# Attention stage of a two-layer hybrid block: a third score buffer, and two PSUM banks for everything else

## The chip, the core and the metric

The kernel runs on one core of a Trainium2 chip. The core has TensorE (PE in the profile; PEld is its weight load), VectorE (DVE), ScalarE (ACT), GpSimd (POOL) and SyncE (SP, which issues the loads and stores here). They run side by side, each through its own queue in order, and wait for each other by semaphores. PE writes its results into PSUM, eight banks of 512 fp32 columns by 128 partitions; DVE and ACT read them from there. The metric is the device time of one execution in microseconds (us), lower is better.

## What is computed

Two layers over 512 latent and 256 context tokens of width 1024. The part that matters here is the attention of head group B (four heads, two softmax maps each) and the output projection behind it, which also takes the results of groups A and C:

```
def diff_attn(q, k, v, lam):
    s = jnp.einsum("bqhmd,bkhmd->bhmqk", q.astype(F32), k.astype(F32)) * (B_QK_DIM ** -0.5)
    p = jax.nn.softmax(s, axis=-1)
    a = p[:, :, 0] - lam * p[:, :, 1]
    return jnp.einsum("bhqk,bkhd->bqhd", a, v.astype(F32))
...
def mixer_merge(pa, o, pc, P, lam_init):
    ya = chunk_gmlp(pa, P)
    yb = (rms_norm(o, P["subln_g"]) * (1.0 - lam_init)).astype(pa.dtype).reshape(b, n, B_WIDTH)
    yc = conformer_conv(pc, P)
    return jnp.concatenate([ya, yb, yc], axis=-1) @ P["w_out"]
...
    x_lat = x_lat + g1 * mixer_merge(pa, o, pc, P, lam_init)
```

Latent queries see 768 keys (latent and context); context queries, in layer 0 only, see the 256 context keys.

## The kernel before

Each layer goes through four stages: input projections with groups A and C; attention with the first part of the output projection; the rest of the output projection with the second norm; the gated feed-forward network. The change is in the attention stage (lines 766 to 922).

**Units and pairs.** A pair is one head with 256 queries, a unit one half of it (128 queries). Layer 0 has four small pairs on the context (256 keys) and eight large ones (768 keys), layer 1 the eight large ones. `q_prep` turns the queries of a pair on PE (tile `pq`) and splits them into a high part `qh` (ACT and POOL) and a remainder `ql` (DVE; the tile is called `qlz`). `scores` makes two score tiles per unit, one for each softmax map: four matmuls into `pss` (two banks, 1024 columns), then the row maximum on DVE (L825) and the exponential with its sum on ACT (L97, tile `e`). `combine` joins the two maps on DVE (L841). `transp` turns the result in blocks of 128 on PE into `pat` (a tile of four blocks and one of two), which ACT (L858) and DVE (L860) copy to `ath`. `attn_v` multiplies with the values into `po` (L870), and `subln` makes the norm's sum on PE (`pr`, L882), two small ACT steps and the scaled result `yB`, again as a high part and a remainder. Units are staggered: the transposes come two units behind the scores, `po` three, `pr` five.

**Fills.** The output projection sums over the results of A and C (`yAC`) and of B (`yB`). The share of `yAC` is known before the attention. So for `NFILL` = 2 (layer 0) and 3 (layer 1) blocks of 256 output columns, `wout` with parts (0,) computes it inside the attention stage: groups of twelve matmuls (four blocks of the sum, three products of high and low parts each, lines 275 to 277) into a bank `wo`, then one DVE update of the residual `xT` (L758). The segments are the 256 context tokens (layer 0 only) and the 512 latent ones, so a matmul of a fill has 256 or 512 columns. They come last in the program's text, so a scheduler that goes by priority puts them where PE would otherwise have nothing ready. The first group of layer 0 is written ahead of the attention. Their weights are loaded by SP and split into a high part `whi` (ACT) and a remainder `wlo` (POOL or DVE) in two buffers each; the first two blocks of layer 1 may come split already from DRAM (`wh`, `wl`).

**PSUM.** Eight banks: two score buffers of two banks (tag "s"), three banks for `pq`, `pat`, `po` and `pr` (tag "w", `WB`), one for the fills (tag "f", `FB`). A tile waits until the last reader of its bank's previous tile is done.

The order of each engine's instructions is set before the run by the scheduler, from priorities and free buffers; on the chip each engine goes through it strictly.

Of the kernel before, what the change touches and what calls it, by code (L numbers as in the profile page):

```python
# [9 lines left out]
F32 = mybir.dt.float32  # L10
# [6 lines left out]
P = 128  # L17
# [27 lines left out]

FB, WB, EB, QB = 1, 3, 5, 3
MRB, MRW, RAWB, NSQ, NTB, KXB, FTB = 4, 2, 3, 2, 3, 3, 2

HP, SCP, RSP = 1000, 2, 60
# [25 lines left out]
def tile_backbone(  # L77
# [18 lines left out]
    def act(out, in_, func, **kw):  # L96
        r = S.activation(out, in_, func, **kw)  # L97
        tab["since"].append(r.ins)
        tc.add_manual_dep(r.ins, tab["load"].name, NOSYNC, reason="activation table order")
        return r  # L100
# [13 lines left out]
    def psum_pool(stack, name):  # L114
        return stack.enter_context(tc.tile_pool(name=name, bufs=1, space=PSUM, reuse_waits="tile"))
# [99 lines left out]
    def wsplit(src, shape, eng="mix", raw=None, p=None, tags=("hi", "lo"), bufs=2):  # L215
        raw = raw or wload(src, shape)
        hi, lo = [(p or wp).tile([P] + shape, F32R, tag=t, name="w" + t, bufs=bufs) for t in tags]
        lo_n[0] += 1
        with tc.high_priority(offset=400):
            S.copy(hi, raw)  # L220
            e = V if eng == "dve" else G if eng == "pool" or lo_n[0] % 2 else V
            sub_lo(lo, raw, hi, e)
        return hi, lo
# [39 lines left out]
    def wsplit_of(key, src, shape, eng, tags=("hi", "lo"), p=None, **kw):  # L263
        if key not in split:
            return wsplit(src, shape, eng, p=p, **kw)
        r = []
        for x, t in enumerate(tags):
            w = (p or wp).tile([P] + shape, F32R, tag=t, name="w" + "hl"[x], bufs=RAWB if t == "raw" else 2)
            flat = w.rearrange("p a n -> p a n") if len(shape) == 2 else w.rearrange("p a k m -> p a (k m)")
            nc.sync.dma_start(out=flat.bitcast(F32), in_=split[key][:, x])  # L270
            r.append(w)
        return r

    def mm3(o, lhi, llo, rhi, rlo, start, stop):
        T.matmul(o, lhi, rhi, start=start, stop=False)  # L275
        T.matmul(o, lhi, rlo, start=False, stop=False)  # L276
        T.matmul(o, llo, rhi, start=False, stop=stop)  # L277
# [54 lines left out]
    for l in range(DEPTH):  # L332
# [5 lines left out]
        whole = [GL] if last else [GC_, GL]  # L338
# [20 lines left out]
        with ExitStack() as ph:  # L359
            sac = ExitStack()  # L360
            sp = pool(sac, f"s1_{l}", side)
            ps = psum_pool(ph, f"ps1_{l}")
# [380 lines left out]
        def wout_w(mp2, parts, eng, **kw):  # L743
            return [(wsplit_of(("out", q, mp2), w_out[l, q, mp2], [2, 4, P], eng, **kw), (yACh, yACl) if q == 0 else (yBh, yBl))
                    for q in parts]

        def wout(mp2, parts, w, segs, psf, tag, bufs, only=(0, 1)):

            for g in segs:
                a, b, s = g  # L750
                for i in only:
                    m = 2 * mp2 + i
                    o = psf.tile([P, 512], F32, tag=tag, name="wo", bufs=bufs)
                    for n, ((wh, wl), (yh, yl)) in enumerate(w):
                        for k in range(4):
                            mm3(o[:, :b - a], wh[:, i, k], wl[:, i, k], yh[:, k, a:b], yl[:, k, a:b],
                                n == 0 and k == 0, n == len(w) - 1 and k == 3)
                    V.scalar_tensor_tensor(  # L758
                        out=xT[:, m, a:b], in0=o[:, :b - a], scalar=modv[:, l, s, 2, m:m + 1],
                        in1=xT[:, m, a:b], op0=ALU.mult, op1=ALU.add)  # L760
                    if 1 in parts:
                        for h in ngs:
                            if h[0] >= a and h[1] <= b:
                                norm.add(m, h)

        with ExitStack() as ph:
            sp = pool(ph, f"s2_{l}", side)
            ps = psum_pool(ph, f"ps2_{l}")
# [16 lines left out]
            def q_prep(n):  # L785
                h, p = pairs[n]
                qh = sp.tile([P, 2, 256], F32R, tag="qh", name="qh", bufs=QB)
                ql = qlz[n % 2]
                pq = ps.tile([P, 256], F32, tag="w", name="pq", bufs=WB)
                for i in range(2):  # L790
                    T.transpose(pq[:, i * P:(i + 1) * P], qt[2 * p + i][:, h * P:(h + 1) * P], ident)
                if n == 0:
                    for m in range(2):
                        for a in range(2):
                            S.copy(qh[a * QKD:(a + 1) * QKD, m], pq[m * QKD:(m + 1) * QKD])
                    for m in range(2):
                        ms = slice(m * QKD, (m + 1) * QKD)
                        sub_lo(ql[ms, m], pq[ms], qh[ms, m])
                else:
                    qn = sp.tile([P, 256], F32R, tag="qn", name="qn", bufs=2)  # L800
                    S.copy(qn, pq)
                    for m in range(2):
                        src = qn[m * QKD:(m + 1) * QKD]
                        for a in range(2):
                            (G.tensor_copy if a else S.copy)(qh[a * QKD:(a + 1) * QKD, m], src)
                    for m in range(2):
                        ms = slice(m * QKD, (m + 1) * QKD)
                        sub_lo(ql[ms, m], pq[ms], qn[ms])
                st["q", n] = (qh, ql)

            def scores(n, i):
                h, p = pairs[n]
                k0, nk = (0, 6) if p < 2 else (LAT, 2)
                qh, ql = st["q", n]
                e = []
                sm = sp.tile([P, 2], F32, tag="sm", name="sm", bufs=4)
                for m in range(2):
                    pss = ps.tile([P, 1024], F32, tag="s", name="pss", bufs=2)
                    for (a, b) in ([(0, 512), (512, 768)] if p < 2 else [(0, 256)]):
                        ksl = slice(k0 + a, k0 + b)  # L820
                        qs = slice(i * P, (i + 1) * P)
                        T.matmul(pss[:, a:b], qh[:, m, qs], kk[:, 2 * h + m, ksl], start=True, stop=False)
                        T.matmul(pss[:, a:b], ql[:, m, qs], kk[:, 2 * h + m, ksl], start=False, stop=True)  # L823
                    mx = sp.tile([P, 1], F32, tag="mx", name="mx", bufs=4)
                    V.tensor_reduce(out=mx, in_=pss[:, :nk * P], op=ALU.max, axis=AX.X, negate=True)  # L825
                    em = sp.tile([P, TOK], F32, tag="e", name="e", bufs=EB)
                    act(em[:, :nk * P], pss[:, :nk * P], AF.Exp, bias=mx, accum_out=sm[:, m:m + 1])
                    e.append(em)
                st[n, i] = (e, sm)
# [61 lines left out]
            if l == 0:  # L891
                w0 = wout_w(0, (0,), "pool")
                g, i = first.pop(0)
                wout(0, (0,), w0, [g], ps, "f", FB, (i,))
            q_prep(0)
            nu = len(units)
            for u in range(nu + 8):
                if u < nu:
                    n, i = units[u]
                    if i == 0 and n + 1 < len(pairs):  # L900
                        with tc.high_priority(offset=SCP):
                            q_prep(n + 1)
                    with tc.high_priority(offset=SCP):
                        scores(n, i)
                    combine(n, i)
                v = u - LAG[0]
                if 0 <= v < nu:
                    transp(*units[v])
                v = u - LAG[1]
                if 0 <= v < nu and units[v][1] == 1:  # L910
                    attn_v(units[v][0])
                v = u - LAG[2]
                if 0 <= v < nu and units[v][1] == 1:
                    subln(units[v][0])

            for mp2 in range(NFILL[l]):
                if mp2 == 0 and l == 0:
                    for g, i in first:
                        wout(0, (0,), w0, [g], ps, "f", FB, (i,))
                else:  # L920
                    wout(mp2, (0,), wout_w(mp2, (0,), "pool"), whole, ps, "f", FB)
        kvs.close()


# [9 lines left out]
        with ExitStack() as ph:  # L934
            pss_ = ctx.enter_context(ExitStack())
            ps = psum_pool(pss_, f"ps3_{l}")
# [18 lines left out]
            for x in range(len(todo) + 1):  # L955
# [3 lines left out]
                if x < len(todo):  # L959
                    mp2, w, i = todo[x]  # L960
# [8 lines left out]
        with ExitStack() as ph:  # L969
# [22 lines left out]
            for half in range(2):  # L992
                gh = hp.tile([P, HJ, toks], F32R, tag="gh", name="gh", bufs=1)
                gl = hp.tile([P, HJ, toks], F32R, tag="gl", name="gl", bufs=1)
                for jj in range(HJ):
# [3 lines left out]
                    w = [wsplit(w_gv[l, j, g], [KD, P], "dve") for g in range(2)]  # L999
# [43 lines left out]
                for mp2 in range(KD // 2):  # L1043
                    tail = half == 1 and mp2 == KD // 2 - 1
                    ws = {}
                    for gi, gs in enumerate([[g] for g in ngs] if tail else [whole]):
                        pd = {g: [ps.tile([P, 512], F32, tag="acc", name="pd", bufs=8) for i in range(2)] for g in gs}
                        cs_ = chunks[::-1] if gi else chunks
                        for ci, (j0, jn) in enumerate(cs_):
# [4 lines left out]
                            for jj in range(jn):  # L1054
# [3 lines left out]
                                for g in gs:  # L1058
                                    a, b, s = g
# [4 lines left out]
                        for g in gs:  # L1064
                            a, b, s = g
# [109 lines left out]
```

## Time and profile before

| | |
|---|---|
| median of 3 runs | 1602.82 us (1602.46 to 1603.99) |
| the profiled execution | 1602.73 us, of which its span 1600.4 |
| PE busy in the span | 1565.2 us (98%), 8186 matmuls |
| DVE busy | 1016.0 us (63%) |
| ACT busy | 643.3 us (40%) |
| POOL busy | 113.3 us (7%) |
| attention of layer 0, from the first pq to the last pr | 244.3 to 349.2 us |
| attention of layer 1 | 1108.8 to 1191.7 us |

The span runs from the first to the last instruction. A matmul's row shows its own duration, which overlaps the next one's; the step from one start to the next is what PE spends on it. DVE and ACT rows overlap a little in the same way. In a row of the timeline, brackets at the end name idle time just before it and what ended it.

### The profile page before, as it was taken

To read this page: it belongs to the slowest core of one execution; us is meant where nothing else is said; L and a number is where in the kernel's file an instruction comes from. 1 tells how busy PE (TensorE), PEld (TensorE's weight loads), DVE (VectorE), ACT (ScalarE), POOL (GpSimd) and SP (SyncE) were. 2 spreads that over 40 slices of the span, in tenths; PEclk is the share of its full clock that TensorE was granted. 3 is DMA by queue.
4 is the path that set the end of the run, shared out by engine and by line. 5 is a ranking of instruction groups with operands and counts; after the bars stand their busy time and mean duration, and the time that the engine had idled before them with its cause. 6 is when DMAs were issued, how large, how long until landed. Compare 5 with 4: busy or idle time off the path is not lost.

```text
span 1600.4 us, 21118 instructions
## 1 busy us (share of the span) xinstructions
PE 1565.2 (98%) x8186; PEld 1289.8 (81%) x8186; DVE 1016.0 (63%) x1713; ACT 643.3 (40%) x1115; POOL 113.3 (7%) x128
## 2 busy tenths in 40 slices
PE   6999998999999999999999999999999999999999
PEld 4875776778788888888888887887778888888888
DVE  4497968969999982145444354996977444334433
ACT  5431568762532221124333233255765333123321
POOL 1130124310000000000000000001320000000000
PEclk9999999999999999999999999999999999999999
DMA  7625210015265872116666476642011323332232
GB/s 282 216 68 183 62 54 27 14 40 198 68 196 185 284 257 74 63 66 198 209 192 207 152 272 221 202 157 93 14 42 54 103 95 96 89 103 92 92 108 90
DMA packets 76372, 208.77 MB, mean 130 GB/s; under 512 B 11504, under 2 KB 13808, under 8 KB 76144
## 3 DMA queue, kind: packets, MB, share of 16 engines
q1 hardware_dynamic: 76272, 207.43, 40.0%
q8 instruction: 64, 1.05, 0.3%
q14 instruction: 36, 0.29, 0.1%
HBM read 183.28 MB, written 24.12 MB: 130 GB/s over the span
## 4 chain that ended last, share of the span: by engine, by line
PE 91%; DVE 4%; ACT 4%; issue 1%; DMA 0%; POOL 0%; POOLq 0%; DVEq 0%; SPq 0%; ACTq 0%
PE pp L276 13%; PE pp L275 13%; PE pp L277 13%; PE pd L277 6%; PE pd L276 6%; PE pd L275 6%; PE acc L443 5%; PE acc L451 5%; PE acc L444 5%; PE po L870 3%; PE wo L275 2%; PE wo L276 2%; PE wo L277 2%; PE mr L156 2%; ACT e L97 1%; PE accC L496 1%
## 5 line engine op out<-in xcount | busy, mean ns | idle before, releaser
L220 ACT CAST whi<-raw 128x1024 fp32r<-128x1024 f32 (+1 forms) x174 | 178.4, 1027 | 510.3 <-PE pp L276 248.4
L276 PE MATMUL pp<-hlo,whi 128*128 128x512 f32 (+1 forms) x1072 | 380.6, 356 | 0.8 <-DVE hlo L316 0.8
L275 PE MATMUL pp<-hhi,whi 128*128 128x512 f32 (+1 forms) x1072 | 379.8, 356 | 1.5 <-ACT whi L220 1.3
L277 PE MATMUL pp<-hhi,wlo 128*128 128x512 f32 (+1 forms) x1072 | 379.0, 355 | 0.0
L106 DVE TENSOR_TENSOR wlo<-raw,whi 128x1024 fp32r<-128x1024 f32 (+2 forms) x159 | 191.4, 1206 | 287.9 <-ACT whi L220 280.3
L275 PEld LDWEIGHTS pp<-hhi,whi 128*128 128x128 f32 x1072 | 201.3, 188 | 35.2 <-ACT whi L220 2.7
L276 PEld LDWEIGHTS pp<-hlo,whi 128*128 128x128 f32 x1072 | 201.4, 188 | 32.8 <-DVE hlo L316 1.5
L277 PEld LDWEIGHTS pp<-hhi,wlo 128*128 128x128 f32 x1072 | 201.7, 188 | 30.9
L277 PE MATMUL pd<-gh,wlo 128*128 128x512 f32 (+1 forms) x550 | 193.2, 351 | 0.0
L276 PE MATMUL pd<-gl,whi 128*128 128x512 f32 (+1 forms) x550 | 192.5, 350 | 0.0
L275 PE MATMUL pd<-gh,whi 128*128 128x512 f32 (+1 forms) x550 | 191.8, 349 | 0.0
L275 PEld LDWEIGHTS pd<-gh,whi 128*128 128x128 f32 x550 | 103.4, 188 | 15.0
L276 PEld LDWEIGHTS pd<-gl,whi 128*128 128x128 f32 x550 | 103.3, 188 | 15.1
L277 PEld LDWEIGHTS pd<-gh,wlo 128*128 128x128 f32 x550 | 103.7, 189 | 14.4
L701 DVE SCALAR_TENSOR_TENSOR cacc<-cin,cw,cacc 128x783 f32<-128x783 f32 (+1 forms) x120 | 103.4, 913 | 3.4 <-ACT cacc L696 3.4
L1037 DVE TENSOR_TENSOR ft<-ft,pp 128x256 f32<-128x256 f32 (+1 forms) x66 | 39.4, 598 | 95.9 <-PE pp L277 84.4
L192 DVE CUSTOM_DVE_ANT_0 mraw<-mraw,csil,bmod 128x1024 f32<-128x1024 f32 x64 | 81.7, 1279 | 7.2 <-DMA mraw<-in_w_modT_dram 7.1
L97 ACT ACTIVATE ft<-ft 128x768 f32<-128x768 f32 (+1 forms) x44 | 32.6, 740 | 112.4 <-DVE ft L1032 112.3
L443 PE MATMUL acc<-whi,hhi 128*128 128x512 f32 x192 | 77.7, 405 | 0.0
L444 PE MATMUL acc<-whi,hlo 128*128 128x512 f32 x192 | 77.0, 401 | 0.0
L97 ACT ACTIVATE e<-pss,mx 128x768 f32<-128x768 f32 (+1 forms) x80 | 65.1, 816 | 16.8 <-DVE mx L825 15.0
L825 DVE TENSOR_REDUCE mx<-pss 128x1 f32<-128x768 f32 (+1 forms) x80 | 67.3, 845 | 5.6 <-PE pss L823 4.6
(218 smaller groups left out, 2522.1 us busy)
## 6 DMA issues: line engine op xcount, KB each, us to landing
raw<-in_w_gv_dram SPq DMA_DIRECT2D x88, 512.0 KB, 3.2
mraw<-in_w_modT_dram SPq DMA_DIRECT2D x64, 512.0 KB, 4.3
raw<-in_w_down_dram SPq DMA_DIRECT2D x34, 512.0 KB, 3.6
wh<-in SPq DMA_DIRECT2D x24, 512.0 KB, 4.7
wl<-in SPq DMA_DIRECT2D x24, 512.0 KB, 4.5
raw<-in_w_in_dram SPq DMA_DIRECT2D x20, 512.0 KB, 3.9
araw<-in_w_in_dram SPq DMA_DIRECT2D x40, 256.0 KB, 3.6
in<-ahi SPq DMA_DIRECT2D x40, 256.0 KB, 4.7
```

What stands on the lines that cost most here:

```text
L97: r = S.activation(out, in_, func, **kw)
L106: (eng or V).tensor_sub(o, a, hi.bitcast(F32))
L192: r = V.tensor_tensor_reduce(out=junk, in0=w, in1=csil[:, s], scale=1.0, scalar=bmod[:, l, i, f:f + 1], op0=ALU.mult, op1=ALU.add, accum_o ...
L220: S.copy(hi, raw)
L275: T.matmul(o, lhi, rhi, start=start, stop=False)
L276: T.matmul(o, lhi, rlo, start=False, stop=False)
L277: T.matmul(o, llo, rhi, start=False, stop=stop)
L443: T.matmul(pt[t], hhi[hs], wh[:, a], start=k2 + a == 0, stop=False)
L444: T.matmul(pt[t], hlo[hs], wh[:, a], start=False, stop=False)
L451: T.matmul(pt[t], hhi[hs], wl[:, a], start=False, stop=k2 + 1 == KD // 2 and a == 1)
L701: V.scalar_tensor_tensor(out=cacc[:, c, :cn], in0=cin[:, c, j:j + cn], scalar=cw[:, l, c, j:j + 1], in1=cacc[:, c, :cn], op0=ALU.mult, op1 ...
L825: V.tensor_reduce(out=mx, in_=pss[:, :nk * P], op=ALU.max, axis=AX.X, negate=True)
```

## The change

The fills lose their own bank and take tag "w"; `WB` goes from three banks to two; the scores get a third buffer of two banks. That is again eight banks.

```diff
-FB, WB, EB, QB = 1, 3, 5, 3
+WB, EB, QB = 2, 5, 3
...
-                    pss = ps.tile([P, 1024], F32, tag="s", name="pss", bufs=2)
+                    pss = ps.tile([P, 1024], F32, tag="s", name="pss", bufs=3)
...
-                wout(0, (0,), w0, [g], ps, "f", FB, (i,))
+                wout(0, (0,), w0, [g], ps, "w", WB, (i,))
...
-                        wout(0, (0,), w0, [g], ps, "f", FB, (i,))
+                        wout(0, (0,), w0, [g], ps, "w", WB, (i,))
...
-                    wout(mp2, (0,), wout_w(mp2, (0,), "pool"), whole, ps, "f", FB)
+                    wout(mp2, (0,), wout_w(mp2, (0,), "pool"), whole, ps, "w", WB)
```

No instruction is added or taken away; the scheduler's order changes in the attention stages and just behind them. Three places show how. Tiles carry their numbers, and "waits" names the engines whose semaphores a row waits for.

First, PE in a pair in the middle of layer 1. Before, from the query transposes on:

```order
L791 MATMUL pq_10241<-ident_62,q2_9110 128x128 [waits Activation_49]
L791 MATMUL pq_10241<-ident_62,q3_9111 128x128
L277 MATMUL wo_10635<-yACh_8536,wlo_10632 128x512
L275 MATMUL wo_10635<-yACh_8536,whi_10631 128x512
L276 MATMUL wo_10635<-yACl_8537,whi_10631 128x512
L822 MATMUL pss_10253<-kk_9106,qh_10139 128x512 [waits Activation_49,Pool_49]
L823 MATMUL pss_10253<-kk_9106,qlz1_9784 128x512
L822 MATMUL pss_10253<-kk_9106,qh_10139 128x256
L823 MATMUL pss_10253<-kk_9106,qlz1_9784 128x256
L109 MATMUL pat_10278<-ident_62,e_10159 128x128 [waits DVE_49,Activation_49]
L109 MATMUL pat_10278<-ident_62,e_10159 128x128 x3
L277 MATMUL wo_10635<-yACh_8536,wlo_10632 128x512
```

Now, in the same pair, behind pq_10241 and pat_10278, up to the result po_10288:

```order
L822 MATMUL pss_10308<-kk_9106,qh_10139 128x512 [waits Activation_49]
L823 MATMUL pss_10308<-kk_9106,qlz1_9784 128x512
L822 MATMUL pss_10308<-kk_9106,qh_10139 128x256
L823 MATMUL pss_10308<-kk_9106,qlz1_9784 128x256
L822 MATMUL pss_10317<-kk_9106,qh_10139 128x512 [waits PE_49,Activation_49]
L823 MATMUL pss_10317<-kk_9106,qlz1_9784 128x512
L822 MATMUL pss_10317<-kk_9106,qh_10139 128x256
L823 MATMUL pss_10317<-kk_9106,qlz1_9784 128x256
L109 MATMUL pat_10284<-ident_62,e_10159 128x128 [waits Activation_49]
L109 MATMUL pat_10284<-ident_62,e_10159 128x128
L870 MATMUL po_10288<-ath_10176,vt_9107 128x256 [waits DVE_49]
L870 MATMUL po_10288<-ath_10176,vt_9107 128x256 x5
```

The fills (wo) are gone from between. The next unit's scores, pss_10308 and pss_10317, stand ahead of po_10288; before, they stood behind it and its norm. pat_10284 and po_10288 each wait for one of the two banks.

Second, ACT around its copy of pat_10278. Before:

```order
L801 CAST qn_10244<-pq_10241 128x256 [waits PE_49]
L805 COPY qh_10240<-qn_10244 64x256 [waits Activation_49]
L805 COPY qh_10240<-qn_10244 64x256
L858 COPY ath_10277<-pat_10278 128x4x128 [waits PE_49]
L97 ACTIVATE e_10223,sm_10206<-pss_10216,mx_10221 128x768 [waits DVE_49]
L97 ACTIVATE e_10260,sm_10252<-pss_10253,mx_10258 128x768 [waits DVE_49]
L873 COPY o_10295<-po_10288 128x256 [waits PE_49]
```

Now:

```order
L97 ACTIVATE e_10223,sm_10206<-pss_10216,mx_10221 128x768 [waits DVE_49]
L887 CAST yBh_9773<-o_10093 128x256 [waits DVE_49]
L801 CAST qn_10244<-pq_10241 128x256 [waits PE_49]
L97 ACTIVATE e_10260,sm_10252<-pss_10253,mx_10258 128x768 [waits DVE_49]
L805 COPY qh_10240<-qn_10244 64x256 [waits Activation_49]
L805 COPY qh_10240<-qn_10244 64x256
L858 COPY ath_10277<-pat_10278 128x4x128 [waits PE_49]
```

The copy of pat_10278 has moved behind two exponentials, e_10223 and e_10260.

Third, PE at the end of layer 1's attention. Before:

```order
L882 MATMUL pr_10583<-osq_10550,ones_64 128x256 [waits PE_49,Pool_49]
L277 MATMUL wo_10669<-yACh_8536,wlo_10666 128x512
L275 MATMUL wo_10669<-yACh_8536,whi_10665 128x512
L276 MATMUL wo_10669<-yACl_8537,whi_10665 128x512
L277 MATMUL wo_10669<-yACh_8536,wlo_10666 128x512
L882 MATMUL pr_10590<-osq_10579,ones_64 128x256 [waits Pool_49]
L275 MATMUL wo_10683<-yACh_8536,whi_10665 128x512 [waits DVE_49]
```

Now:

```order
L882 MATMUL pr_10583<-osq_10550,ones_64 128x256 [waits PE_49,Pool_49]
L882 MATMUL pr_10590<-osq_10579,ones_64 128x256 [waits Pool_49]
L275 MATMUL wo_10601<-yACh_8536,wh_10597 128x512 [waits DMAHW6_49,Activation_49]
L276 MATMUL wo_10601<-yACl_8537,wh_10597 128x512
L277 MATMUL wo_10601<-yACh_8536,wl_10599 128x512 [waits DMAHW7_49]
L275 MATMUL wo_10601<-yACh_8536,wh_10597 128x512
```

Behind the last norm there stood the last group of the fills; now the first group, and all others of the layer follow it. Layer 0 ends in the same way.

## Rows read from the trace of the kernel before

**Rows 1.** Waits of PE in the whole span: total us, times, longest us.

```profile
PE pss L822 <- ACT e L97: 5.7, 8, 1.1
```

**Rows 2.** Stretches of five (layer 0) and four (layer 1) pairs: busy us per engine.

```profile
286.30:334.70 48.40, 45.85 (x260) 38.76 (x260) 45.64 (x84) 37.72 (x88) 15.66 (x23) 1.00 0.03 12
1139.00:1175.20 36.20, 35.38 (x194) 29.24 (x193) 32.83 (x62) 27.84 (x67) 10.74 (x18) 1.00 0.00 1
```

**Rows 3.** Timeline of PE: start us, us; four norms (pr), one result (po).

```profile
286.35 0.59 PE L882 MATMUL pr<-osq,ones 128*128 128x256 f32 x2
...
334.67 0.59 PE L882 MATMUL pr<-osq,ones 128*128 128x256 f32 x2
...
1136.48 2.75 PE L870 MATMUL po<-ath,vt 128*128 128x256 f32 x12
1139.07 0.59 PE L882 MATMUL pr<-osq,ones 128*128 128x256 f32 x2
...
1175.21 0.59 PE L882 MATMUL pr<-osq,ones 128*128 128x256 f32 x2
```

**Rows 4.** Stretches, instructions on the tile wo alone: busy us (count).

```profile
244.45:348.88 104.43, 19.33 (x76) 11.73 (x76) 4.11 (x7) 0.97 0.03 11
1108.80:1191.30 82.50, 19.24 (x60) 10.33 (x60) 3.62 (x5) 1.00 0.08 27
1139.07:1175.21 36.14, 6.07 (x18) 3.02 (x18) 0.73 (x1) 1.00 0.00 1
```

**Rows 5.** Timeline of PE: first and last of 12 fills; second and last.

```profile
242.85 0.28 PE L275 MATMUL wo<-yACh,whi 128*128 128x256 f32 x1
...
244.16 0.28 PE L277 MATMUL wo<-yACh,wlo 128*128 128x256 f32 x1
...
1192.08 0.39 PE L276 MATMUL wo<-yACl,whi 128*128 128x512 f32 x1
...
1194.37 0.39 PE L277 MATMUL wo<-yACh,wlo 128*128 128x512 f32 x1
```

**Rows 6.** Timeline of DVE in a pair of layer 1.

```profile
1150.78 1.02 DVE L841 SCALAR_TENSOR_TENSOR e<-e,cc 128x768 f32<-128x768 f32 x1
1151.71 0.42 DVE L106 TENSOR_TENSOR yBl<-o,yBh 128x256 fp32r<-128x256 f32 x1
1152.05 0.95 DVE L825 TENSOR_REDUCE mx<-pss 128x1 f32<-128x768 f32 x1
1152.91 0.42 DVE L860 COPY ath<-pat 128x256 f32<-128x256 f32 x1
1153.24 0.95 DVE L825 TENSOR_REDUCE mx<-pss 128x1 f32<-128x768 f32 x1
```

**Rows 7.** Timeline of ACT in the same pair.

```profile
1152.19 0.82 ACT L805 CAST qh<-qn 64x256 fp32r<-64x256 f32 x2
1152.92 0.57 ACT L858 COPY ath<-pat 128x512 f32<-128x512 f32 x1
1153.52 0.90 ACT L97 ACTIVATE e<-pss,mx 128x768 f32<-128x768 f32 x1
...
1154.41 0.89 ACT L97 ACTIVATE e<-pss,mx 128x768 f32<-128x768 f32 x1
```

**Rows 8.** Timelines of PE and DVE: first and last use of one pq tile.

```profile
1141.58 0.38 PE L791 MATMUL pq<-ident,q 128*128 128x128 f32 x2
...
1146.69 0.43 DVE L106 TENSOR_TENSOR qlz<-pq,qn 64x256 fp32r<-64x256 f32 x1
```

**Rows 9.** Timeline of DVE behind the last scores of layer 1.

```profile
1179.33 1.22 DVE L106 TENSOR_TENSOR wlo<-raw,whi 128x1024 fp32r<-128x1024 f32 x1
...
1180.80 0.95 DVE L825 TENSOR_REDUCE mx<-pss 128x1 f32<-128x768 f32 x1
```

**Rows 10.** Stretches of layer 0's first units: busy us, PEclk after POOL.

```profile
250.00:252.00 2.00, 0.93 (x6) 0.76 (x6) 2.00 (x8) 1.59 (x8) 0.47 (x1) 1.00 0.00 0
254.00:256.00 2.00, 1.20 (x5) 1.24 (x6) 0.97 (x4) 1.79 (x7) 1.24 (x3) 0.50 0.00 0
```

## Prediction

> **What bounds the kernel now.** Over the whole span TensorE (PE) is the bound: 1565.2 of 1600.4 us busy. A change to the attention stage can therefore pay in two ways only: by closing PE's gaps, or by letting more of PE's work lie beside the other engines. I read the waits of PE first. The line that answers to a third score buffer is a score matmul waiting for ScalarE's exponential to release one of the two buffers: 5.7 us in all, eight times [rows 1]. That is the whole direct prize.
>
> Next, the two attention stages cut into stretches. In five pairs of layer 0 PE is busy 45.85 of 48.40 us and VectorE (DVE) 45.64; in four pairs of layer 1 it is 35.38 and 32.83 of 36.20, with ScalarE (ACT) at 27.84 [rows 2]. So PE and DVE are both near full. The starts of the norm matmuls give the pace: 286.35 to 334.67 is five pairs, **9.66 us each**; 1139.07 to 1175.21 is four, **9.03 us each** [rows 3].
>
> Last, what PE does in those stages. Between the start of the attention and the last norm it executes 76 matmuls of the output projection in layer 0 and 60 in layer 1 [rows 4]: the fills. They sit in PE's queue where it would otherwise wait for DVE or ACT. In layer 1's four pairs there are 18. At 0.229 us a step (1192.08 to 1194.37, ten steps) [rows 5] they are 4.1 us, so PE's own work is (35.38 - 4.1) / 4 = 7.8 us a pair, and DVE's, without the one update of xT (0.73), is (32.83 - 0.73) / 4 = 8.0 [rows 2, 4].
>
> **The change, part by part.** *The fills lose their bank.* They now take the tag of the transposes, and the order of instructions shows every one of them behind the last norm, in both layers; only the first twelve of layer 0 stay ahead of the stage. What moves is exactly the 76 and 60. Layer 0: 36 with 256 columns (three segments of twelve) at 0.119 us (242.85 to 244.16, eleven steps) and 40 with 512 columns at 0.229 us [rows 4, 5]: 4.3 + 9.2 = **13.5 us**. Layer 1: 60 x 0.229 = **13.7 us**. Behind the last norm there is nothing left for PE to wait for, so these lie on the path in full. Their updates of xT on DVE (seven take 4.11 us, five 3.62 [rows 4], so 0.6 to 0.7 us each) lie beside the next twelve matmuls of 1.4 or 2.7 us, in the other of two banks, and cost nothing; without that cover each would cost its 0.7 us. Their weights are loaded and split ahead of the stage, as now; GpSimd's queue loses no step. On SyncE's queue the loads behind them shift: five in a row of the output projection's weights, not seven, go out ahead of the modulation's, which comes back under the seams.
>
> *What the stage gives back.* This is the uncertain term: how long is a pair without fills, with three score buffers, but two instead of three banks for the transposes (pat), the query transpose (pq), the result (po) and the norm (pr)? I walked one pair of layer 1 through the new order with steps from the trace. DVE: maximum 0.87 us, combine 0.93, copy 0.33 [rows 6]. ACT: exponential with its accumulator 0.89, copy of a transpose 0.55, the two halves of qh 0.8 [rows 7]. PE: po 2.6 (1136.48 to 1139.07) [rows 3], a score buffer 0.7 (two matmuls of 0.229 us, two of 0.119), six transposes 0.6 (an estimate: six of at most 0.119 us).
>
> Put the end of a po at 0. The norm and three of four matmuls of the next scores run to 0.85, pat_10230 and pat_10236 to 1.45, the next scores and pq_10241 to 2.3. pat_10278 needs the bank of pat_10230. ACT reads po first, then three small norm steps, then copies pat_10230 at 1.7 to 2.3; pat_10278 and the rest of the scores run to 2.8. pss_10308 needs the exponential behind that copy (to 3.1) and runs to 3.85. pss_10317 needs the next exponential, whose maximum DVE gives at 3.3, and ACT has two casts ahead of it: 4.8. So PE stands for 1.0 us and runs to 5.55. pat_10284 needs the bank of pat_10278, and in the new order ACT's copy of it stands **behind** that exponential and both halves of qh: 6.3. PE stands again for 0.85 us. Then pat_10284 to 6.6 and po to **9.2**. The second pair, walked on, comes to 9.0. I take **9.1 us a pair**. The third score buffer's gain is eaten: its wait is replaced by a wait for one of two banks. Behind the stalled pat in PE's queue are po, pr and the next pair's scores, for which DVE's maxima wait in turn.
>
> From both sides: not below DVE's own 8.0 us; and not above 11.1, if the banks are held as long as now. One pq bank is held today from 1141.58 to 1147.12, 5.5 us [rows 8]; in my walk it is 3.5 (2.3 to 5.8), so the difference is 2.0 us a pair. 9.1 is nearest to what both layers show today.
>
> With 9.1 over the steady pairs: layer 0 (9.66 - 9.1) x 5 = -2.8 us; layer 1 (9.1 - 9.03) x 4 = +0.3 us. I leave the start of each stage as it is: in both orders the first scores need ql, which DVE makes from the first pq, and no fill stands ahead of that.
>
> *Seams.* The first fill waits until ACT has read a norm out of one of two banks: about 0.5 us in each layer (one short ACT step, 0.4 [rows 7], and the hand-over). In layer 0 the second set of weights behind the fills can only be split when the fills let go of their buffer; PE has 14 matmuls of 0.119 us (1.7 us) until it needs the difference, which takes a cast and 1.22 us [rows 9]: I put 0.8 us, from 0 to 1.5. On the other side, in layer 1 a weight difference of 1.22 us now stands on DVE right ahead of the maximum of the last scores [rows 9]. It cannot be there any more, since the fills hold both buffers of the split weights: -1.2 us.
>
> *Sum:* 13.5 - 2.8 + 1.3 + 13.7 + 0.3 + 0.5 - 1.2 = **+25.3 us**. On the profiled execution's own 1602.7 us, which is the median of the runs (1602.82) within 0.1, that is **1628 us**, 1.6% slower. Its own range, from pairs of 8.6 to 9.6 us, is 1624 to 1633.
>
> **Rivals.** *A: DVE sets the pace.* If the third buffer and the absent fills keep DVE dense, a pair takes 8.0 us. Then the steady pairs give back 1.66 x 5 + 1.03 x 4 = 12.4 us in place of 2.5, and the time is 1618; over all eight large pairs of each layer 21.5 us, 1609. For it speaks DVE's share (94% and 91% of the stretches [rows 2]); against it, the walk's bank waits.
>
> *B: two banks are far too few.* With pairs of 11.1 us the sum is 27.8 + 1.44 x 5 + 2.07 x 4 = +43 us, 1646. For it speaks how long pq is held [rows 8]; against it, the walk, in which pq is let go earlier.
>
> *C: the clock falls.* In layer 0's first units PE is 47% busy from 250 to 252, and from 254 to 256 its granted clock is 0.50, the lower of the two levels (1.2 in place of 2.4 GHz) [rows 10]. Without fills PE waits more, above all at the stage's end, where only transposes and results are left; if the clock falls there, the first 7 us of fills in each layer cost up to 3.5 us more: +7, 1635. The Trainium skill (TensorE: Matmul & The Clock Gate, What's actually happening) says that the throttled state is the default and activity lifts it. The trace agrees in this one place; the busier stretches of [rows 2] keep 1.00.
>
> *D, the other side: the gap closes and the fills cost nothing.* If the score buffers are what holds the stage, a third one takes away PE's 5.7 us [rows 1], and the time is 1602.7 - 5.7 = 1597 us. For that the stage must shrink by as much as the fills cost behind it. Without the pace terms the sum is 27.8 us, over sixteen large pairs 1.74 each, so it is even only at 7.6 us a pair or less. But DVE's own work is 8.0 and PE's 7.8 [rows 2, 4]: both would have to shrink. The Trainium skill (Perfetto Trace Analysis, Optimization Strategy) says that the same gap repeating on the engine that should be saturated can mean that there isn't enough PSUM for the next tile. The trace agrees that this gap is a buffer's; what the banks taken for it cost, the rule leaves open.
>
> **How the numbers follow.** My forecast, +21 to +30 us, has 0.60; A 0.18; B 0.11; C 0.08; D 0.03. Predicted is 1628 us. The range reaches into A (down to 1612) and past C (to 1641) and leaves out B's far end, A's far end and D, some 2 in 10. About 0.2%, 3 us, is what a measurement of this kernel can tell from no change; faster by more 0.02, within it 0.02, slower 0.96: only D ends on that side.
>
> **What would show it.** In the new profile all wo rows stand behind the last pr, the first of them some 0.5 us after it, in runs of 0.229 and 0.119 us. The norms of steady pairs are about 9.1 us apart in both layers, PE is about 85% busy there, and its waits name ACT's copies of transposes (ath) and DVE's ql in place of the exponentials. If pairs are 8.0 to 8.5 us apart, A holds; above 10, B; a granted clock of 0.5 after 270 us, C. The prediction is wrong if fills appear among the scores, or if the pairs fall below 8.

## The result, and the profile after

The changed kernel takes **1620.19 us** (median of four runs, 1619.92 to 1621.24) beside 1602.88 for the kernel before (1602.46 to 1603.99): a ratio of 1.0108, 95% interval 1.0091 to 1.0126. It is 1.1% slower; 1628 us was forecast, in a range from 1612 to 1641. The profiled execution took 1620.36 us with a span of 1618.6, so 18.2 us more than the span before.

The timeline of PE in the new profile answers to [rows 3] and [rows 5] (start us, us; the bracket is idle time before the instruction and what ended it):

```profile
287.61 0.59 PE L882 MATMUL pr<-osq,ones 128*128 128x256 f32 x2
...
322.95 0.59 PE L882 MATMUL pr<-osq,ones 128*128 128x256 f32 x2
...
329.88 0.59 PE L882 MATMUL pr<-osq,ones 128*128 128x256 f32 x2
...
343.63 0.70 PE L882 MATMUL pr<-osq,ones 128*128 128x256 f32 x2 [1.33 <-POOL osq L875]
343.98 0.47 PE L275 MATMUL wo<-yACh,whi 128*128 128x256 f32 x1
...
362.43 0.39 PE L277 MATMUL wo<-yBh,wlo 128*128 128x256 f32 x1 [1.17 <-DVE wlo L106]
...
1147.86 0.59 PE L882 MATMUL pr<-osq,ones 128*128 128x256 f32 x2
...
1174.03 0.59 PE L882 MATMUL pr<-osq,ones 128*128 128x256 f32 x2
...
1180.89 0.59 PE L882 MATMUL pr<-osq,ones 128*128 128x256 f32 x2
...
1194.70 0.70 PE L882 MATMUL pr<-osq,ones 128*128 128x256 f32 x2 [1.33 <-POOL osq L875]
1195.05 0.58 PE L275 MATMUL wo<-yACh,wh 128*128 128x512 f32 x1
...
1212.68 0.47 PE L275 MATMUL wo<-yACh,whi 128*128 128x512 f32 x1 [0.94 <-ACT whi L220]
```

The fills stand behind the last norm in both layers, as forecast, and the first of them (343.98 and 1195.05) follows that norm without a wait. The same five pairs of layer 0 now take 42.27 us and the same four of layer 1 33.03: 8.45 and 8.26 us a pair, where 9.1 was forecast and 9.66 and 9.03 stood before [rows 3]. These means hide a difference. The last pair of each stretch takes only 6.93 and 6.86 us (from 322.95 and from 1174.03): PE executes 39 matmuls in it, no query transposes, since no further pair follows, and 12 score matmuls in place of 16. The full pairs ahead of it take 8.84 us (287.61 to 322.95, four pairs) and 8.72 us (1147.86 to 1174.03, three).

The stretches behind that are, first, these pairs (they answer to [rows 2]), then each layer from its first query transpose (pq) to the first matmul of the second half of the output projection (yBh), then the first units (they answer to [rows 10]); the columns are us, busy us of PE, PEld, DVE, ACT, POOL with counts, PEclk, DMA share, GB/s:

```profile
287.61:329.88 42.27, 39.82 (x217) 32.59 (x216) 41.07 (x77) 34.81 (x87) 15.79 (x23) 1.00 0.00 1
1147.86:1180.89 33.03, 31.42 (x172) 25.66 (x171) 31.98 (x61) 27.30 (x69) 12.24 (x18) 1.00 0.00 1
243.87:360.87 117.00, 102.26 (x531) 82.31 (x529) 98.86 (x206) 83.30 (x220) 39.09 (x63) 0.96 0.07 26
1117.16:1215.50 98.34, 86.24 (x437) 68.52 (x436) 76.73 (x139) 65.89 (x151) 28.27 (x44) 1.00 0.06 19
...
250.00:256.00 6.00, 4.63 (x18) 3.98 (x19) 4.74 (x17) 4.08 (x17) 2.08 (x5) 0.50 0.00 0
```

The kernel before, from the same first pq to the same first yBh, then the first 16 us of layer 1's stage and the same first units of layer 0:

```profile
244.28:353.81 109.53, 98.78 (x531) 80.65 (x530) 93.06 (x193) 85.14 (x220) 38.13 (x63) 0.97 0.03 10
1108.79:1197.32 88.53, 83.59 (x437) 67.75 (x436) 76.51 (x140) 67.18 (x152) 28.76 (x44) 1.00 0.07 25
...
1108.79:1124.79 16.00, 14.57 (x77) 11.23 (x75) 14.39 (x27) 13.05 (x30) 7.48 (x14) 1.00 0.11 35
...
250.00:256.00 6.00, 3.85 (x19) 3.31 (x20) 4.87 (x17) 4.38 (x17) 2.16 (x5) 0.71 0.00 0
```

With the norms as marks, each layer falls into three parts, and the sum of the prediction can be set beside them (layer 0 / layer 1, us):

| part | forecast | measured |
|---|---|---|
| first pq to the first norm of the steady pairs | 0 / 0 | 42.07 to 43.74, +1.67 / 30.28 to 30.70, +0.42 |
| the five / four steady pairs | -2.8 / +0.3 | -6.05 / -3.11 |
| from there to the first yBh: last pairs, fills, seams | +14.0 / +13.0 | 19.14 to 30.99, +11.85 / 22.11 to 34.61, +12.50 |
| wait for wlo behind it | +0.8 | +1.17 |
| sum | +25.3 | +18.45, beside 18.2 of the span |

The pairs make most of the difference. Last, the waits of PE, which answer to [rows 1] (total us, times, longest):

```profile
PE pss L822 <- ACT e L97: 12.2, 22, 1.4
...
PE pat L109 <- ACT ath L858: 2.9, 5, 1.0
...
PE pat L109 <- DVE e L841: 2.3, 2, 1.4
```

The wait that the third buffer should take away, 5.7 us before, has grown to 12.2. And the one that was to take its place, for ScalarE's copies of the transposes, is 2.9 us in all.

### The profile page after: what moved, and what is told of

The parts are those of the page before. It is cut to its first block, busy times and chain, and to the rows that moved or that the text cites. A ratio compares the mean times of both kernels' runs of the same rounds, so it can differ in the third digit from the quotient of the medians.

```text
span 1618.6 us, 21119 instructions
## 1 busy us (share of the span) xinstructions
PE 1571.9 (97%) x8186; PEld 1293.3 (80%) x8186; DVE 1017.0 (63%) x1713; ACT 640.9 (40%) x1115; POOL 113.8 (7%) x128
## 3 DMA queue, kind: packets, MB, share of 16 engines
q1 hardware_dynamic: 76272, 207.43, 38.9%
## 4 chain that ended last, share of the span: by engine, by line
PE 88%; DVE 6%; ACT 4%; issue 1%; DMA 1%; POOL 0%; DVEq 0%; SPq 0%; ACTq 0%; POOLq 0%
PE pp L276 13%; PE pp L275 13%; PE pp L277 13%; PE pd L277 6%; PE pd L276 6%; PE pd L275 6%; PE acc L443 5%; PE acc L451 5%; PE acc L444 5%; PE po L870 3%; ACT e L97 2%; PE wo L275 2%; PE wo L276 2%; PE mr L156 2%; PE wo L277 2%; PE accC L496 1%
## 5 line engine op out<-in xcount | busy, mean ns | idle before, releaser
L822 PE MATMUL pss<-kk,qh 128*128 128x256 f32 (+1 forms) x144 | 57.9, 406 | 14.3 <-ACT e L97 12.2
```

## The experiments

The forecast's own reason for the pairs is **T2**: two banks for transposes, results and norms set the pace, and the third buffer's gain is eaten. The first rival was **T1**: VectorE's own work sets the pace of a pair, which is rival A. Behind the first four runs came two more pairs of theories. **T3**: the fills' place is what costs, and the third buffer gives a good part back; against **T4**: the loss is the third bank taken from the rest. **T6**, against T1: no engine sets the pace alone, but the chain of score, maximum, exponential and free buffer does. **T7**, against T3: PE is so full in the kernel before that the fills lengthen its pairs.

**The third buffer alone (e1).** In the changed kernel:

```diff
-pss = ps.tile([P, 1024], F32, tag="s", name="pss", bufs=3)
+pss = ps.tile([P, 1024], F32, tag="s", name="pss", bufs=2)
```

> The changed kernel without its third score buffer: two score buffers, two banks for the rest, fills behind the stage as in the changed kernel; two of the eight banks stay empty. T1 (VectorE's own work, some 8.5 us, sets the pace of a pair; the third buffer only keeps VectorE fed): VectorE runs dry where it did before, pairs of 8.8 to 9.2 us, 1622 to 1627 us. T2 (the two banks of transposes, results and norms set the pace, and the third buffer's gain is eaten): nothing changes, 1619 to 1621 us.

Measured: 1637.78 us, ratio to the kernel before 1.022 (1.0203 to 1.0237). Without its third buffer the changed kernel is 17.6 us slower. Neither interval holds: the buffer is worth far more than both theories said, and T2's "nothing changes" is out.

**Two more banks for the rest (e2), one more (e5).** Both have two score buffers, and the fills behind the stage:

```diff
-WB, EB, QB = 2, 5, 3
+WB, EB, QB = 4, 5, 3
...
-pss = ps.tile([P, 1024], F32, tag="s", name="pss", bufs=3)
+pss = ps.tile([P, 1024], F32, tag="s", name="pss", bufs=2)
```

> The changed kernel with the two banks of the third score buffer given to the transposes, results, norms and fills instead (two score buffers, four such banks). T1: as with two such banks and two score buffers, within 3 us of the run beside it. T2: with four banks the waits for a bank go, pairs fall from 8.7 towards 8.0 us, 1608 to 1612 us.

Measured: 1624.86 us, 1.0141 (1.0126 to 1.0157). Two more banks for transposes and results are worth 12.9 us over e1, so with two score buffers these banks do hold the pairs, against T1. But T2's 1608 to 1612 us are not reached, and the same two banks do more as a third score buffer.

With three such banks it is the kernel before except for the fills, which is their move alone:

> The fills' move alone: score buffers (two) and the three banks of the rest as in the kernel before, but the fills take the tag of the transposes and so stand behind the stage; one of eight banks stays empty. T3 (the fills' place costs some 28 us, which the third score buffer then gives back in part by closing bank waits): between the versions with two and with four such banks, 1627 to 1633 us. T4 (the move itself is cheap, and the loss is the third bank taken from the rest): 1600 to 1608 us.

Measured: 1635.6 us, 1.0201 (1.0186 to 1.0217): +32.4 us. T4 is out. It lies 2.6 us above T3's interval, nearer to the version with two such banks than to the one with four. Its steady pairs:

```profile
287.66:334.62 46.96, 40.84 (x220) 33.03 (x218) 40.74 (x78) 35.78 (x87) 15.78 (x23) 1.00 0.00 1
1156.59:1194.48 37.89, 32.83 (x175) 27.51 (x174) 33.65 (x62) 28.55 (x69) 10.14 (x18) 0.95 0.00 1
```

Without the fills the nine pairs together are not shorter (84.85 us instead of 84.46), and behind the norms the fills are paid.

**The fills left out (e12).** In the kernel before:

```diff
-for mp2 in range(NFILL[l]):
-    if mp2 == 0 and l == 0:
-        for g, i in first:
-            wout(0, (0,), w0, [g], ps, "f", FB, (i,))
-    else:
-        wout(mp2, (0,), wout_w(mp2, (0,), "pool"), whole, ps, "f", FB)
+for mp2 in range(1 - l, NFILL[l]):
+    wout_w(mp2, (0,), "pool")
```

> The kernel before without its fills behind the first segment (84 matmuls of layer 0 and 72 of layer 1 with their updates of xT are left out; some 31.6 us of PE by 0.227 and 0.119 us a step; the weights are still loaded and split). T3 (the fills cost nothing where they stand among the scores, apart from the 20 that lie behind the last norm): 1595 to 1605 us. T7 (PE is so full that the fills lengthen the pairs by about half of their time): 1580 to 1590 us.

Measured: 1607.87 us, 1.0039 (1.0024 to 1.0054). With 31.6 us of PE's work left out the kernel is not faster but 5.6 us **slower**. T7 is out, and T3's interval is passed by 2.9 us. Stretches of this version, its steady pairs and the start of layer 1:

```profile
290.65:337.60 46.95, 40.82 (x220) 33.01 (x218) 40.74 (x78) 35.80 (x87) 15.66 (x23) 1.00 0.00 1
1146.11:1184.26 38.15, 33.06 (x176) 27.59 (x175) 33.65 (x62) 28.57 (x69) 10.43 (x18) 0.96 0.00 1
...
1112.28:1128.28 16.00, 12.82 (x40) 9.26 (x40) 13.03 (x23) 11.06 (x25) 4.33 (x9) 0.57 0.27 88
```

Without fills the five pairs are 1.4 us shorter (46.95 instead of 48.32) and the four 2.0 us longer (38.15 instead of 36.14): before, the fills lay in time in which PE would have stood. As in e5, they cost nothing among the scores.

That this version is slower still has another cause, at the start of the stages. From the first query transpose to the first norm of the steady pairs it takes 47.18 us in layer 0 and 33.83 in layer 1, instead of 42.07 and 30.28 before. The missing fills explain little of that: e5 has none there either and takes 43.45 and 30.48. In e12 no fill holds the buffers of the split weights, and ACT splits two further weights ahead of the first queries. PE's first query transposes and first score of layer 0 with ACT's split between them, in e12:

```profile
243.47 0.82 PE L791 MATMUL pq<-ident,q 128*128 128x128 f32 x6
...
244.75 1.99 ACT L220 CAST whi<-raw 128x1024 fp32r<-128x1024 f32 x2 [1.93 <-POOL wlo L106]
...
247.44 0.58 PE L822 MATMUL pss<-kk,qh 128*128 128x256 f32 x1 [3.15 <-ACT qh L795]
```

And in e5:

```profile
244.21 1.18 PE L791 MATMUL pq<-ident,q 128*128 128x128 f32 x6
245.42 0.38 PE L822 MATMUL pss<-kk,qh 128*128 128x256 f32 x1
```

The first score comes 3.97 us behind the first query transpose instead of 1.21. In layer 1 it comes 2.54 us behind it, and in the first 16 us of that stage the clock is 0.57; the kernel before was granted 1.00 there. So the 5.6 us are for the most part not what the missing fills cost. How they divide between the splits and the clock was not measured.

Who waits for the scores tells what time the fills lay in. The lines of the view of the tile pss below say what PE's score matmuls waited for, and then who waited for them (us, times). In the kernel before:

```profile
  ACT e L97: 5.7, 8
...
  DVE mx L825: 4.6, 12
```

In the same kernel without its fills (e12):

```profile
  ACT e L97: 12.4, 17
...
  DVE mx L825: 17.8, 30
```

With the fills behind and two score buffers, first with three banks (e5), then with two, which is the changed kernel without its third buffer (e1):

```profile
  ACT e L97: 13.5, 19
...
  DVE mx L825: 14.7, 24
```

```profile
  ACT e L97: 16.2, 23
...
  DVE mx L825: 16.5, 23
```

In the changed kernel:

```profile
  ACT e L97: 12.2, 22
...
  DVE mx L825: 2.3, 5
```

Without fills among the scores, PE's wait for a free score buffer is 12 to 16 us in these versions, and it does not go away with a third one. What the third one changes is that VectorE's maxima no longer wait for scores: 16.5 us in e1, 14.7 in e5, 2.3 in the changed kernel. That is 14.2 us of waiting beside the 17.6 us between the times of e1 and the changed kernel, and 12.4 beside 15.4 for e5.

**VectorE's work cut (e3), moved (e8), added (e9).** All three in the changed kernel; e3 and then e8 and e9:

```diff
-V.scalar_tensor_tensor(out=e0, in0=e1, scalar=cc, in1=e0, op0=ALU.mult, op1=ALU.add)
+V.scalar_tensor_tensor(out=e0[:, :P], in0=e1[:, :P], scalar=cc, in1=e0[:, :P], op0=ALU.mult, op1=ALU.add)
```

```diff
-    V.tensor_copy(at[osl], pat[:, :cn_])
+    S.copy(at[osl], pat[:, :cn_])
```

```diff
 V.scalar_tensor_tensor(out=e0, in0=e1, scalar=cc, in1=e0, op0=ALU.mult, op1=ALU.add)
+V.tensor_copy(junk, e1[:, :256])
```

> The changed kernel with VectorE's combine cut: the second softmax map is subtracted over 128 of the 768 keys only, the rest of that subtraction is left out. That is some 0.7 us less of VectorE for each of two combines of a pair. T1: pairs fall by 0.7 to 1.4 us (to PE's own 7.8, if that is right), over sixteen pairs 11 to 22 us: 1598 to 1609 us. T2: the bank waits stay, the time stays within 4 us of 1620.

> The changed kernel with the copy of the second group of transposes on ScalarE in place of VectorE: VectorE is relieved of two times 0.33 us a pair, ScalarE (81 per cent busy) gets as much. T1 (VectorE sets the pace, 97 per cent busy): pairs fall by 0.3 to 0.5 us before PE's own work holds them, 1612 to 1616 us. Rival (the chain over ScalarE's exponentials and copies sets it): pairs get longer, 1622 to 1628 us.

> The changed kernel with one more copy on VectorE in each unit (256 columns of the second exponential's tile into a tile that nobody reads), by the rows some 0.3 to 0.4 us, so 0.6 to 0.8 us a pair. T1 (VectorE sets the pace): over sixteen pairs 10 to 13 us more, 1630 to 1633 us. T6 (no single engine sets it, the chain of score, maximum, exponential and free buffer does): half of that or less, 1621 to 1626 us.

Measured: e3 1615.66 us, 1.0085 (1.007 to 1.01); e8 1623.15 us, 1.0126 (1.0111 to 1.0141); e9 1628.2 us, 1.0167 (1.0152 to 1.0183). T1 fails in e3 and in e8. A combine shorter by 0.7 us takes off 4.5 us, not 11 to 22; T2's line for this run, within 4 us of 1620, is narrowly missed too. The moved copy gains nothing: 3.0 us slower by the medians, with intervals that overlap, and inside the rival's 1622 to 1628 us. In e9 the sum lies between the two theories, and the pairs decide. The five and the four steady pairs of e9, then the first units of layer 0 in e9 and in the changed kernel:

```profile
293.25:335.11 41.86, 39.18 (x215) 32.37 (x214) 41.56 (x88) 34.74 (x87) 19.14 (x23) 1.00 0.00 1
1156.95:1190.64 33.69, 31.53 (x171) 25.77 (x170) 33.11 (x70) 27.57 (x69) 15.24 (x18) 1.00 0.01 1
244.66:293.25 48.59, 38.81 (x166) 28.59 (x165) 39.97 (x105) 35.84 (x106) 20.88 (x36) 0.82 0.04 12
...
243.87:287.61 43.74, 34.62 (x164) 26.63 (x163) 38.17 (x91) 35.46 (x106) 20.30 (x36) 0.88 0.04 13
```

In five pairs VectorE got ten copies more, and they are 0.4 us **shorter** than without; its busy share rose from 97 to 99%. The four of layer 1, with eight copies more, are 0.7 us longer. Together 18 copies of 0.27 us, 4.9 us, lengthen the nine pairs by 0.3 us. The groups of VectorE's instructions in those five pairs show where it fits in. Of the changed kernel:

```profile
L841 DVE SCALAR_TENSOR_TENSOR e<-e,cc 128x768 f32<-128x768 f32 x10 | 10.5, 1046 | 0.3
...
L885 DVE SCALAR_TENSOR_TENSOR o<-o,gsub,osq 128x256 f32<-128x256 f32 x5 | 3.2, 644 | 0.3 <-ACT osq L97 0.2
```

And of e9:

```profile
L842 DVE SCALAR_TENSOR_TENSOR e<-e,cc 128x768 f32<-128x768 f32 x10 | 10.0, 1004 | 0.0
...
L843 DVE COPY junk<-e 128x256 f32<-128x256 f32 x10 | 2.7, 273 | 0.0
L887 DVE SCALAR_TENSOR_TENSOR o<-o,gsub,osq 128x256 f32<-128x256 f32 x5 | 2.4, 485 | 0.0
```

The same operation on the same shape is recorded 644 ns long in one and 485 in the other. So recorded durations are not fixed: without the ten copies (2.7 us) VectorE's busy time in e9 is 38.9 us, 2.2 less than the 41.07 of the changed kernel for the same work. That a part of the 97% was time in which an instruction had begun and was not getting on is a reading of this; no run shows it. What e9 costs lies for the most part elsewhere: of the 10.0 us between the two profiled spans 4.9 are in the first units of layer 0, 48.59 us instead of 43.74, at a clock of 0.82 where the changed kernel has 0.88.

**The same test on ScalarE (e10) and PE (e11).** The copy goes to ScalarE, and in e11 the first four transposes are made twice:

```diff
+S.copy(junk, e1[:, :256])
```

```diff
 flip(pat[:, c], e[:, (c0 + c) * P:(c0 + c + 1) * P])
+if c0 == 0:
+    flip(pat[:, c], e[:, (c0 + c) * P:(c0 + c + 1) * P])
```

> The same extra copy of 256 columns in each unit, on ScalarE in place of VectorE (some 0.4 us, 0.8 us a pair). T1: ScalarE has a fifth of its time free, so within 4 us of the changed kernel, 1618 to 1624 us. T6: ScalarE's copies stand between the exponentials that free the score buffers, so as much as on VectorE or more, 1624 to 1633 us.

> The changed kernel with the first four transposes of each unit made twice (the second time over the first), which adds eight transposes of some 0.1 us to PE in a pair, 0.8 us. T1: PE has 0.6 to 1 us a pair free, so at most a third of it shows, 1620 to 1625 us. T6: PE's transposes lie between the scores, and nearly all of it shows, 1628 to 1633 us.

Measured: e10 1625.04 us, 1.0144 (1.0127 to 1.0161); e11 1622.65 us, 1.0131 (1.0116 to 1.0146). The five pairs of e10, and those of e11:

```profile
290.62:334.92 44.30, 40.13 (x220) 32.80 (x219) 41.40 (x79) 38.78 (x97) 16.73 (x23) 1.00 0.00 1
```

```profile
287.02:331.00 43.98, 43.34 (x258) 35.83 (x257) 41.77 (x79) 35.40 (x87) 14.37 (x23) 1.00 0.00 1
```

Of the three engines ScalarE has the most free time (34.81 busy of 42.27 us), and yet added work shows on it at least as much as on PE: ten copies of 0.41 us, 4.1 us, make the five pairs 2.0 us longer. On PE some 40 transposes make them 1.7 us longer. In the whole time the copies on ScalarE cost 4.9 us, inside T6's interval, and the transposes 2.5, inside T1's. With e3, e8 and the pairs of e9 the weight lies with T6. That it is this chain, and which step of it is the longest, was not shown by a run of its own.

**The fills between the units (e4).** The changed kernel's banks, with the fills written out inside the loop:

```diff
                     subln(units[v][0])
+                if fills and u >= 5 and u % 2 == 1:
+                    fill()
```

> The changed kernel's banks (three score buffers, two banks for the rest), but the fills are written out inside the loop over units, one in every second unit, so that they take their turn among the transposes and norms. T1: PE has room for a part of them beside VectorE's 8.5 us a pair (PE's own 7.8), so that some 0.7 us a pair, 11 us in all, are hidden: 1605 to 1612 us. T2: each fill holds one of two banks for over 3 us, pairs go above 10 us, 1625 to 1640 us.

Measured: 1616.92 us, 1.0092 (1.0077 to 1.0107), between the two intervals: 3.3 us less than the changed kernel, with intervals that overlap. The four pairs of layer 1, all instructions and then those on the tile wo alone:

```profile
1146.92:1190.57 43.65, 42.61 (x222) 34.05 (x220) 36.94 (x67) 30.98 (x71) 12.76 (x19) 1.00 0.08 25
...
1146.92:1190.57 43.65, 12.45 (x48) 8.70 (x48) 3.01 (x4) 1.00 0.08 25
```

48 fills of 0.229 us are 11.0 us, and the pairs are 10.6 us longer than without. Written as blocks of eleven or twelve into a bank that the transposes wait for, the fills are paid almost in full; it is not enough that they stand in the stage. Which of the two, the block or the shared bank, does it was not separated.

**Three buffers and the fills' own bank (e6, e7).** e6 is the kernel before with three score buffers and one bank for the rest; e7 lays three buffers of 768 columns end to end in one tile of five banks, so that two banks remain for the rest and one for the fills:

```diff
-FB, WB, EB, QB = 1, 3, 5, 3
+FB, WB, EB, QB = 1, 1, 5, 3
```

```diff
+pk = ps.tile([P, 2560], F32, tag="s", name="pk", bufs=1)
...
-pss = ps.tile([P, 1024], F32, tag="s", name="pss", bufs=2)
+pss = pk[:, x * 768:(x + 1) * 768]
```

> Three score buffers, and of the two banks left one for transposes, results and norms and one for the fills, which so can stand among the scores again. T3: the fills are hidden again, but one bank holds pq, four pats, po and pr one after the other, by the rows some 10 to 10.5 us a pair: 1612 to 1630 us, the last norm of each layer later than in the changed kernel and only a few fills behind it. T4: one bank instead of two is worse than the changed kernel by far, over 1640 us.

> Three score buffers of 768 columns laid end to end in five banks (the middle one starts in the middle of a bank), which leaves two banks for transposes, results and norms and one for the fills: the changed kernel's buffers, and the fills' own bank of the kernel before. T3: the fills are hidden again and the third buffer closes waits: 1592 to 1600 us. T4 (two banks for the rest are what costs): 1606 to 1620 us.

Measured: e6 1672.64 us, 1.0434 (1.0416 to 1.0451); e7 1717.06 us, 1.0711 (1.0695 to 1.0727). With one bank for all, the five pairs of layer 0 take 70.56 us (303.97 to 374.53), 14.1 each, where 10 to 10.5 were worked out, and T4's line for this run holds: taking the second bank away as well costs 52 us over the changed kernel. e7 lies far outside both intervals and decides nothing between them. PE waits in it 33 times for an exponential:

```profile
PE pk L827 <- ACT e L97: 41.3, 33, 2.1
```

The three parts of one tile are not used as three buffers: scores wait for the exponentials of their neighbours. Whether that is the bookkeeping of the one tile or the shared banks, the run does not tell. What three buffers are worth beside the fills' own bank so stays open, and no version here beat the kernel before.

## Why the prediction was right, and where its sum was off

- **Direction and the fills' price: right.** All fills stand behind the last norm. In layer 1 they run from 1195.05 to 1211.74 (0.94 us ahead of 1212.68): 16.7 us for 72, so 13.9 for the 60 that moved, beside 13.7 forecast. Rival D (1597 us) is out. The pairs of e5 and e12 add what the forecast took for granted: among the scores the same fills cost nothing.
- **The pairs: the step that failed.** "The third score buffer's gain is eaten" put a pair at 9.1 us; the mean is 8.45 and 8.26, with PE 94 to 95% busy, not 85. Over the nine pairs that is -9.2 us instead of -2.5, 6.7 us of a sum that missed by 6.9. Two things are in it. Some 4.4 us come from using 9.1 for the last pair of each stretch, which takes 6.9: a pair with all its scores and a next pair's queries had been walked, and these have neither. The other 2.2 us are the full pairs, 8.84 and 8.72. There the walk had PE stand 0.85 us in each pair for ACT's copy of pat_10278; in the trace the waits of pat for such copies are 2.9 us in the whole span, and two of the five, 1.03 us each, lie behind the steady pairs. What the bank costs does show where there are two score buffers: with two such banks instead of four (e1 against e2) it is 12.9 us. With three buffers the scores run ahead: at the first norm of the steady pairs PE has executed 78 score matmuls in place of 72 (63 in place of 56 in layer 1).
- **The sizing behind it: "the whole direct prize", 5.7 us [rows 1].** That wait was read in a trace in which fills already lay in the gaps. Without them among the scores PE waits 12.4 us and VectorE 17.8 (e12), or 13.5 and 14.7 (e5). The third buffer is worth 15.4 us against the third bank of the rest (e5), 17.6 against nothing (e1).
- **Rivals A and B.** A gives the better total (1618 us), and the mean pair lies within the prediction's own mark for it (8.0 to 8.5); the full pairs, 8.84 and 8.72, do not. Its reason does not hold either: VectorE at 97% took 4.9 us more work for 0.3 us of longer pairs (e9). B's 11.1 us a pair did not come.
- **Rival C** happened in one place: 250 to 256 at 0.50 instead of 0.71, which may be a part of the 1.67 us at the start of layer 0. From 260 us on the clock stayed at 1.00, in the stage's end too.
- **The starts and the seams** nearly cancel, which is luck. The starts, which the forecast left as they were, cost 2.1 us. In layer 1 the units behind the steady pairs, up to the last norm, give back 2.3 us where 1.2 was forecast. No fill waits for a bank (0.5 us forecast in each layer). The wait for wlo is 1.17 us (0.8 forecast); a wait of 0.94 us for whi in layer 1 was not foreseen.

The Trainium skill (Perfetto Trace Analysis, Optimization Strategy) says that where the most contended engine changes from regime to regime, interleaving the regimes may help. This case's trace agrees, with the sign turned round: the change takes such an interleaving apart, and e5 shows 32.4 us for it. The rule on repeating gaps from the same section, cited in the prediction, agrees as well: more PSUM for the scores is worth 15.4 us, though less than the fills that it displaced.

## What to carry to other kernels

A stall that filler work sits in looks small in the profile: before giving the filler's buffer to the stalled stage, ask what the filler will cost when it stands alone, since that is its full length, and what the stall is without it. Filler pays when single instructions of it can slip into gaps out of a buffer of their own; as a block in a shared buffer it was paid almost in full (e4). And a busy share of 97% is no proof that an engine sets the pace: add a known piece of work to it, and look whether the stretch grows.

## What the runs showed of the hardware that was not expected

- A version with less work was granted a lower clock: in e12 it is 0.57 over the first 16 us of layer 1's stage, near the lower of the two levels (1.2 GHz beside 2.4), with 40 matmuls executed; in the kernel before it is 1.00, with 77. The missing fills alone do not explain it: the changed kernel has none in the first 16 us of that stage either, executes 59 matmuls there, and keeps 1.00. In e12 PE also stood 1.71 us before its first query transpose, waiting for the values. The Trainium skill (TensorE: Matmul & The Clock Gate, What's actually happening) says that activity lifts the throttle; this trace agrees.
- Busy time is not fixed for fixed work. PE has 8186 instructions in both profiles, but is busy 1565.2 us before and 1571.9 after, and one VectorE operation lasts 485 or 644 ns in the same place of two kernels.
